# State-space kernel matrices shifted by selecting matmuls on TensorE, with the norm's weights multiplied into x by GpSimd

## Chip, cores and metric

One core of one Trainium2 chip. The metric is the device time of one execution in microseconds (us). Engines are called TensorE (PE in rows, its weight loads PEld), VectorE (DVE), ScalarE (ACT), GpSimd (POOL) and SyncE (SP), which issues most DMAs.

## What is computed

A two-layer encoder trunk on 256 positions of width 2048, in float32. Layer 0 mixes with an S5 state-space model (128 groups of 16 channels, each with 64 complex states), layer 1 with latent attention; each has a gated MLP with a short convolution. Every sub-layer stands between two RMS norms. The change lies in the first mixer:

```python
h = rmsnorm(x, norm_g[0, 0])            # x * rsqrt(mean(x*x) + eps) * g
# s5_mixer, per group of 16 channels:
x_re, x_im = einsum('blgp,gnp->blgn', ub, bb_re), einsum('blgp,gnp->blgn', ub, bb_im)
hs = scan over positions of h[t] = a * h[t-1] + x[t]        # complex, diagonal
y = einsum('blgn,gpn->blgp', hs_re, c_re) - einsum('blgn,gpn->blgp', hs_im, c_im) + d_skip * ub
y = gelu(y)
val, gate = split(y @ w_glu + b_glu, 2)
return val * sigmoid(gate)
```

## The kernel before

All matmuls with large weights split both operands into a rounded part and a remainder and sum three products (`mm3`, L108 to L110); ScalarE makes the rounded part `whi` and VectorE the remainder `wlo` (`split`, L73 and L74), from `raw`, which SyncE loads in pieces of 1 MB. The trunk runs through `s5`, the rest of the GLU, the MLP, attention and the second MLP in one stream; everything behind `s5` is dense in such matmuls.

`s5` cuts the 256 positions into 32 chunks of 8 and works on 8 channel groups at a time: 16 rounds, in a software pipeline. In round n, `part_a` for n + 1 builds on VectorE from powers of the state's eigenvalues (`z`) and the matrices B and C (`bc`) two products f1, f2 (output side) and e1, e2 (input side), each 128x1152 or 128x1024, and sums e1 and e2. B is first multiplied by the norm's weights (`g4`, loaded by SyncE for each round). `part_k` transposes the block of x into `U` (L442), multiplies the last two slices of e1 with f1 and f2 in column tiles of 32 (`tiled`, L399) and so gets one row block `K` of the kernel matrix within a chunk. The matrix within a chunk is a Toeplitz matrix, and its tile `TP` is K shifted by 16 columns for each of 8 rows of blocks. The shift is made by a round trip through DRAM: ScalarE's queue issues a DMA that writes K to `kd` (L460) and, when that has landed, a second one that reads it back with overlapping rows (L463):

```python
act.dma_start(kd.rearrange("r (j w) -> j r w", j=4), K.rearrange("p g c -> p (g c)"))
TPf = TP.rearrange("p j g c -> p (j g c)")[:, : RW - 112]
act.dma_start(TPf, bass.AP(kd.tensor, kd.offset + 16 * RW, [[16, 8], [RW, 16], [1, RW - 112]]))
```

`part_e` transposes e1 into `ET` (8 transposes, L471, copied by ScalarE). In round n + 1, `part_v` multiplies U by ET (L399), ScalarE copies that to `vs`, `part_r` transposes it (L487, L488), rotates it on VectorE (`co`, `si`) and runs the scan over chunks (L498), and `part_h` makes from it the states `H` at the chunks' starts (L503). In round n + 2, `part_c` sums U by TP and H by f1 and f2 into y (L399) and ScalarE applies the GELU into `yg`. After every fourth round `part_d` transposes yg (L540), and from then on each round can take one step of the GLU's matmuls (`glu_early`): 24 matmuls of 128x512, whose sums go to `f` (L256, L258).

At the start X is loaded (8 pieces), ScalarE squares it, GpSimd raises the mean to the power -1/2 (`rstd`, L121), and ScalarE scales X into `act` (`scale_x`, L347). A scheduler lays the instructions of each engine in a fixed order ahead of time; each engine runs its order strictly, and waits on semaphores where an operand isn't there.

## Time and profile before

| what | value |
|---|---|
| runs before, median of 3 | 2263.45 us (2258.99 to 2265.07) |
| the profiled execution, its time and its span | 2263.12 us, 2261.3 us |
| busy: TensorE, weight loads | 2087.9 us (92%), 1769.7 us (78%) |
| busy: VectorE, ScalarE, GpSimd | 1412.9 us (62%), 1095.6 us (48%), 76.5 us (3%) |
[...]
| moved by DMA | 393.28 MB, 174 GB/s |

The span is the time from the first to the last instruction of one profiled execution; its own time is 1.8 us longer. The busy shares are averages over stages that differ: the share of TensorE is far lower in the first 315 us than behind them. [...]

### The profile page before, as it was taken

How to read it: one execution, taken by the hardware profiler on the slowest of the kernel's cores; microseconds unless marked ns; L12 is line 12 of the kernel's file. 1: busy time of each engine (PE TensorE's matmuls, PEld its weight loads, DVE VectorE, ACT ScalarE, POOL GpSimd, SP SyncE). 2: the span in 40 equal slices, each digit the busy share in tenths (PEclk: the TensorE clock that was granted, in tenths of full speed). 3: DMA queues.
4: the chain of work that ended last, by engine and by line, in shares of the span. 5: the costliest groups of instructions: out<-in, count | busy, mean ns of one | idle time of the engine just before them, and what ended most of it. 6: DMA issues, size and time to landing. Idle time of an engine off the chain costs nothing. (4 is left out here: it accounts for less than half of the span.)

```text
span 2261.3 us, 30415 instructions
## 1 busy us (share of the span) xinstructions
PE 2087.9 (92%) x12244; PEld 1769.7 (78%) x12244; DVE 1412.9 (62%) x1904; ACT 1095.6 (48%) x1655; POOL 76.5 (3%) x93
## 2 busy tenths in 40 slices
PE   2576789899999999999998999989999999999997
PEld 1455567688888888888886899878888888888886
DVE  6777756666546655665667666476645655665566
ACT  5454434445545544553454455545545543554444
POOL 0000001200000000000002000120000000000001
PEclk9788899999999999999999999999999999999999
DMA  4455577646555555555555433545555555565554
GB/s 147 108 130 120 131 210 220 184 152 199 184 194 187 186 186 192 188 180 194 193 191 166 135 117 122 189 166 164 185 186 192 186 186 190 190 197 185 189 186 149
DMA packets 285245, 393.28 MB, mean 174 GB/s; under 512 B 9392, under 2 KB 198448, under 8 KB 284080
## 3 DMA queue, kind: packets, MB, share of 16 engines
q1 hardware_dynamic: 280816, 372.60, 50.8%
q10 hardware_dynamic: 4288, 18.74, 3.6%
q8 instruction: 96, 1.57, 0.3%
q14 instruction: 45, 0.37, 0.1%
HBM read 385.29 MB, written 6.03 MB: 173 GB/s over the span
## 5 line engine op out<-in xcount | busy, mean ns | idle before, releaser
L74 DVE TENSOR_TENSOR wlo<-raw,whi 128x1024 fp32r<-128x1024 f32 (+2 forms) x640 | 763.8, 1196 | 590.2 <-ACT whi L73 586.9
L73 ACT ACTIVATE whi<-raw 128x1024 fp32r<-128x1024 f32 (+2 forms) x640 | 658.0, 1031 | 646.5 <-PE wk L114 233.8
L114 PE MATMUL wk<-act,whi 128*128 128x512 f32 x2688 | 944.9, 396 | 0.0
L115 PE MATMUL wk<-act,wlo 128*128 128x256 f32 x2688 | 754.4, 281 | 0.0
L114 PEld LDWEIGHTS wk<-act,whi 128*128 128x128 f32 x2688 | 504.3, 188 | 121.0
L115 PEld LDWEIGHTS wk<-act,wlo 128*128 128x128 f32 x2688 | 507.9, 189 | 0.3
L109 PE MATMUL acc<-wlo,hh 128*128 128x512 f32 x652 | 255.8, 392 | 0.5
L108 PE MATMUL acc<-whi,hh 128*128 128x512 f32 x652 | 255.5, 392 | 0.0
L110 PE MATMUL acc<-whi,hl 128*128 128x512 f32 x652 | 254.4, 392 | 0.0
L109 PEld LDWEIGHTS acc<-wlo,hh 128*128 128x128 f32 x652 | 122.5, 188 | 28.5 <-DVE wlo L74 2.2
L108 PEld LDWEIGHTS acc<-whi,hh 128*128 128x128 f32 x652 | 122.5, 188 | 27.3 <-ACT hh L73 0.5
L110 PEld LDWEIGHTS acc<-whi,hl 128*128 128x128 f32 x652 | 122.5, 188 | 26.9
L109 PE MATMUL acc<-wlo,act 128*128 128x512 f32 (+1 forms) x332 | 129.6, 392 | 4.3 <-DVE wlo L74 4.2
L108 PE MATMUL acc<-whi,act 128*128 128x512 f32 (+1 forms) x332 | 130.0, 395 | 0.8 <-ACT act L73 0.4
L110 PE MATMUL acc<-whi,act 128*128 128x512 f32 (+1 forms) x332 | 127.3, 385 | 0.0
L166 POOL TENSOR_TENSOR f<-f,gb 128x512 f32<-128x512 f32 x24 | 38.1, 1593 | 1901.5 <-issue 1586.3
L109 PEld LDWEIGHTS acc<-wlo,act 128*128 128x128 f32 x332 | 65.0, 196 | 20.1 <-DVE wlo L74 8.2
L755 DVE SCALAR_TENSOR_TENSOR cv<-gs,cw,cv 128x255 f32<-128x255 f32 (+1 forms) x168 | 77.1, 480 | 3.0
L108 PEld LDWEIGHTS acc<-whi,act 128*128 128x128 f32 x332 | 64.7, 197 | 14.9 <-ACT whi L73 1.7
L110 PEld LDWEIGHTS acc<-whi,act 128*128 128x128 f32 x332 | 64.5, 194 | 11.3 <-issue 0.2
L753 ACT ACTIVATE cv<-gs,cb,cw 128x256 f32<-128x256 f32 x84 | 50.4, 601 | 36.7 <-DVE gs L705 36.7
L399 PE MATMUL wk<-TP,U 128*32 128x128 f32 x256 | 20.5, 369 | 47.4 <-DMA TP<-kd 42.5
(281 smaller groups left out, 2377.7 us busy)
## 6 DMA issues: line engine op xcount, KB each, us to landing
raw<-in_w_gate SPq DMA_DIRECT2D x88, 1024.0 KB
raw<-in_w_up SPq DMA_DIRECT2D x88, 1024.0 KB
raw<-in_w_down SPq DMA_DIRECT2D x88, 1024.0 KB
raw<-in_w_glu SPq DMA_DIRECT2D x32, 1024.0 KB
raw<-in_w_o SPq DMA_DIRECT2D x16, 1024.0 KB
TP<-kd ACTq DMA_DIRECT2D x16, 904.0 KB
raw<-in_w_ukv SPq DMA_DIRECT2D x8, 1024.0 KB
gb<-in_norm_g SPq DMA_DIRECT2D x6, 1024.0 KB
```

The costliest lines, as they stand in the source:

```text
L73: act.activation(hi, src, AF.Copy)
L74: (eng or dve).tensor_tensor(lo, src, hi.bitcast(F32), op=ALU.subtract)
L108: pe.matmul(o, lh, rh, start=first, stop=False)
L109: pe.matmul(o, lh, rl, start=False, stop=False)
L110: pe.matmul(o, ll, rh, start=False, stop=last)
L114: pe.matmul(ov, lh, r, start=first, stop=False)
L115: pe.matmul(ov[:, 0, :], ll, r[:, 0, :], start=False, stop=last)
L166: (dve if n == NCH - 1 else pool).tensor_tensor(c, c, g[0][:, n * 512 : (n + 1) * 512], op=ALU.mult)
L399: pe.matmul(o[32 * j : 32 * j + 32, g * P : (g + 1) * P], lhs(g, j), rhs(g, j), start=g == 0 and i == 0, stop=g == NG - 1 and i == len(ter ...
L753: act.activation(cv[:, ft, :], gv[:, ft, :], AF.Identity, scale=cw[:, 2, n : n + 1], bias=cb[:, n : n + 1])
L755: dve.scalar_tensor_tensor(cv[:, ft, sh:], gv[:, ft, : S - sh], cw[:, 2 - sh, n : n + 1], cv[:, ft, sh:], op0=ALU.mult, op1=ALU.add,)
```

## The change

Three edits, all in `s5`.

1. The round trip through DRAM goes. For each of four blocks of 32 columns (j), TensorE multiplies K, taken from a shifted column r, by a constant matrix of zeros and ones that selects 16 of K's rows (`C_SL` in `cst`, which grows from 638 to 894 columns): 2 x 2 x 2 x 4 = 32 matmuls into two banks, in column tiles of 32. ScalarE copies each bank into TP.
2. e1 and e2 are no longer summed on VectorE. `part_e` transposes both by matmuls with the identity that add up in the bank: 16 matmuls in place of 8 transposes. For `part_k` only the last slice is summed on VectorE, into `e7s`, whose other half is zero.
3. The norm's weights no longer go into B and into the skip matrix dB but into X: `gain_x`, 8 products of 128x4x128 on GpSimd in place. The loads of sG and the products with g4 and gX go.

```diff
+            e7s = [T(q1, [P, 8, 2, 16], F32, f"e7{i}", 1) for i in range(2)]
+            for z in e7s:
+                pool.memset(z[:, :, 0, :], 0.0)
...
-            dve.tensor_tensor(dB, dB, gX, op=ALU.mult)
...
+            def gain_x(qt):
+                c = slice(P * qt, P * qt + P)
+                for z in X:
+                    pool.tensor_tensor(z[:, :, c], z[:, :, c], gX[:, c].unsqueeze(1).to_broadcast([P, 4, P]), op=ALU.mult)
+
             def scale_x(rs, qt):
                 c = slice(P * qt, P * qt + P)
+                if qt:
+                    gain_x(qt)
...
-                g4 = T(q1, [P, NP, 16], F32, "g4")
-                sync.dma_start(g4.rearrange("p n q -> p (n q)"), a["sG"][sb].partition_broadcast(P))
-                dve.tensor_tensor(bc4[:, 0:2], bc4[:, 0:2], g4.unsqueeze(1).to_broadcast([P, 2, NP, 16]), op=ALU.mult)
...
-                dve.tensor_tensor(e1, e1, e2, op=ALU.add)
-                return e1, (f1, f2)
+                dve.tensor_tensor(e7s[sb % 2][:, :, 1, :], e1[:, :, 7, :], e2[:, :, 7, :], op=ALU.add)
+                return (e1, e2), (f1, f2)
...
-                    return flat2(e1[:, 4 * g + j, 6:8, :])
+                    return flat2(e7s[sb % 2][:, 4 * g + j])
...
-                act.dma_start(kd.rearrange("r (j w) -> j r w", j=4), K.rearrange("p g c -> p (g c)"))
-                TP = T(q1, [P, 4, NG, 240], F32, "TP")
-                TPf = TP.rearrange("p j g c -> p (j g c)")[:, : RW - 112]
-                act.dma_start(TPf, bass.AP(kd.tensor, kd.offset + 16 * RW, [[16, 8], [RW, 16], [1, RW - 112]]))
+                TP = T(q1, [P, 4, NG * P], F32, "TP")
+                for jj in range(2):
+                    bank = accb()
+                    for j in range(2):
+                        for odd in range(2):
+                            o = C_SL + (2 * (2 * jj + j) + odd) * 32
+                            for b in range(4):
+                                r = 16 * (2 * b + odd)
+                                pe.matmul(
+                                    bank[32 * b : 32 * b + 32, j * 256 : (j + 1) * 256].rearrange("p (g c) -> p g c", g=NG),
+                                    cst[:, o : o + 32], K[:, :, r : r + P],
+                                    start=j == 0 and odd == 0, stop=j == 1 and odd == 1, tile_position=(0, 32 * b),
+                                )
+                    act.activation(TP[:, 2 * jj : 2 * jj + 2, :], bank.rearrange("p (j c) -> p j c", j=2), AF.Copy)
...
-                        pe.transpose(ptv[:, g, :], e1[:, 4 * w + g].rearrange("p s q -> p (s q)"), ident)
+                        for i, z in enumerate(ee):
+                            pe.matmul(ptv[:, g, :], flat2(z[:, 4 * w + g]), ident, start=i == 0, stop=i == 1)
...
             z = [None]
+            gain_x(0)
             rs = first_norm()
```

The scheduler lays the orders anew. Three places show it.

TensorE, one round with a GLU step, from the last `e` tile (L399, now L408) on. In a row stand the bank and, behind the arrow, the moving and the stationary operand. Before:

```order
L110 MATMUL acc_1320<-whi_1315,act_212_925 128x512
...
L399 MATMUL wk_1403<-f_290_1293,e_291_1296 32x128 x4
L471 MATMUL wk_1427<-cst_73,e_291_1296 128x128 x4
L471 MATMUL wk_1433<-cst_73,e_291_1296 128x128 x4
L503 MATMUL wk_1439<-R_1396,cst_73 128x256
L399 MATMUL wk_1501<-ET_1426,U_1401 32x128 x4
L399 MATMUL wk_1513<-TP_1239,U_1216 32x128 x4
```

And of the change:

```order
L408 MATMUL wk_1490<-f_253_1388,e_46_183 32x128 x4
L486 MATMUL wk_1547<-cst_73,e_254_1391 128x128
L486 MATMUL wk_1547<-cst_73,e_255_1392 128x128
...
L472 MATMUL acc_1510<-K_44_179,cst_73 32x256 x16
L472 MATMUL acc_1528<-K_44_179,cst_73 32x256 x16
L486 MATMUL wk_1557<-cst_73,e_254_1391 128x128
...
L518 MATMUL wk_1567<-R_1483,cst_73 128x256
L108 MATMUL acc_1629<-whi_1621,act_214_1162 128x512
```

The selection stands in the middle of the transposed sums, and the GLU's matmuls moved from before the `e` tiles to behind part_h.

ScalarE, a round in which `frames` makes sines (`si`, `co`) for two rounds. Before:

```order
L384 ACT_TABLE_LOAD
L384 ACTIVATE si_1301<-si_1301,cst_73 128x512
L451 ACTIVATE K_44_181<-wk_1218 128x2x112
L472 ACTIVATE ET_1241<-wk_1242 128x512
L460 DMA kd_1237<-K_44_181 4x32x480
L472 ACTIVATE ET_1241<-wk_1248 128x512
L385 ACTIVATE co_1302<-co_1302,cst_73 128x512
L73 ACTIVATE whi_1465<-raw_1463 128x1024
L463 DMA TP_1239<-kd_1237 128x1x1808
L478 ACTIVATE vs_1356<-wk_1347 128x2x128
```

And of the change:

```order
L494 ACTIVATE vs_1858<-wk_1849 128x2x64
L393 ACT_TABLE_LOAD
L393 ACTIVATE si_2022<-si_2022,cst_73 128x512
L539 ACT_TABLE_LOAD
L539 ACTIVATE yg_1253<-wk_1861 128x2x8x16
L450 ACTIVATE U_1903<-wk_1900 128x256
L457 ACTIVATE K_44_179<-wk_1905 128x2x112
L394 ACT_TABLE_LOAD
L394 ACTIVATE co_2023<-co_2023,cst_73 128x512
L487 ACTIVATE ET_1961<-wk_1962 128x512
```

The two DMAs are gone; ahead of K's copy stand a sine, a GELU and two loads of function tables.

GpSimd at the start. Before:

```order
L143 MEMSET st_1736_9994 128x1
L121 ISA
L121 TENSOR_TENSOR rs_y_202<-rs_ms_200,cst_73 128x8
L357 MEMSET z_1261 128x32
L358 MEMSET z_1261 128x32
```

And of the change:

```order
L349 ISA
L349 TENSOR_TENSOR raw_94<-raw_94,gX_104 128x4x128 x4
L349 TENSOR_TENSOR raw_95<-raw_95,gX_104 128x4x128 x2
L121 TENSOR_TENSOR rs_y_205<-rs_ms_203,cst_73 128x8
L349 TENSOR_TENSOR raw_95<-raw_95,gX_104 128x4x128 x2
L366 MEMSET z_1574 128x32
```

Six of the eight products of X with the weights stand ahead of the norm's power, and two behind it.

## Rows read from the trace of the kernel before

**Rows 1.** Windows: us, busy PE, PEld, DVE, ACT, POOL, clock, DMA share, GB/s.

```profile
33.00:104.00 71.00, 39.72 (x544) 29.86 (x545) 49.09 (x82) 26.91 (x64) 0.18 (x2) 0.74 0.47 124
104.00:305.00 201.00, 142.84 (x1455) 108.63 (x1454) 145.00 (x230) 89.88 (x179) 0.22 (x3) 0.82 0.56 133
...
315.00:2261.00 1946.00, 1895.39 (x10164) 1623.84 (x10162) 1188.65 (x1524) 949.94 (x1334) 72.63 (x69) 0.99 0.55 181
```

**Rows 2.** Timeline of VectorE: the scans (L498), one a round; start, duration.

```profile
42.81 0.68 DVE L498 TENSOR_TENSOR_SCAN R<-dc,w 128x256 f32<-128x256 f32 x1
...
103.78 0.69 DVE L498 TENSOR_TENSOR_SCAN R<-dc,w 128x256 f32<-128x256 f32 x1
...
304.51 0.68 DVE L498 TENSOR_TENSOR_SCAN R<-dc,w 128x256 f32<-128x256 f32 x1
```

**Rows 3.** Waits of TensorE from 36 to 320 us: total, times, longest.

```profile
PE wk L399 <- DMA TP<-kd: 42.5, 12, 8.6
PE wk L399 <- ACT ET L472: 15.2, 6, 7.1
PE wk L487 <- ACT vs L478: 15.0, 7, 4.8
```

**Rows 4.** Waits of ScalarE in the same stretch.

```profile
ACT vs L478 <- DMA kd<-K: 22.6, 4, 9.3
ACT bc L420 <- DMA bc<-in_sBC: 21.3, 3, 9.8
```

**Rows 5.** Windows, a stretch in which TensorE waits.

```profile
50.00:55.00 5.00, 0.08 (x4) 0.11 (x8) 0.00 (x0) 0.00 (x0) 0.00 (x0) 0.50 0.45 106
```

**Rows 6.** Timeline of TensorE, a dense stretch.

```profile
158.44 1.08 PE L399 MATMUL wk<-f,e 128*32 128x128 f32 x32
159.46 1.09 PE L471 MATMUL wk<-cst,e 128*128 128x128 f32 x8
160.38 0.38 PE L503 MATMUL wk<-R,cst 128*128 128x256 f32 x1
```

**Rows 7.** Timeline of TensorE from 284 to 296 us.

```profile
286.56 0.60 PE L503 MATMUL wk<-R,cst 128*128 128x256 f32 x2
...
287.23 0.39 PE L109 MATMUL acc<-wlo,act 128*128 128x512 f32 x1
287.46 0.40 PE L110 MATMUL acc<-whi,act 128*128 128x512 f32 x1
...
293.03 0.43 PE L399 MATMUL wk<-TP,U 128*32 128x128 f32 x8 [2.55 <-DMA TP<-kd]
...
294.48 0.50 PE L109 MATMUL acc<-wlo,act 128*128 128x512 f32 x1
```

**Rows 8.** Timeline of VectorE at the start.

```profile
20.99 0.17 DVE L123 TENSOR_TENSOR rs_t<-rs_y 128x8 f32<-128x8 f32 x1 [1.55 <-POOL rs_y L121]
...
25.57 1.35 DVE L430 TENSOR_TENSOR f<-z,bc 128x1152 f32<-128x1152 f32 x1
...
31.64 1.22 DVE L435 TENSOR_TENSOR e<-e,e 128x1024 f32<-128x1024 f32 x1
```

**Rows 9.** Timeline of TensorE at the start: the first `e` tiles.

```profile
32.91 1.93 PE L399 MATMUL wk<-f,e 128*32 128x128 f32 x32 [7.70 <-DVE e L435]
```

**Rows 10.** Groups by line up to 250 us: busy, mean ns of one, idle before.

```profile
L472 ACT ACTIVATE ET<-wk 128x512 f32<-128x512 f32 x26 | 14.8, 594 | 3.8 <-PE wk L471 1.8 <-DVE w L505 1.0 <-DVE w L506 0.4
...
L524 ACT ACT_TABLE_LOAD x5 | 6.4, 1283 | 10.5 <-DMA kd<-K 9.6 <-issue 0.8
...
L418 DVE TENSOR_TENSOR bc<-bc,g 128x256 f32<-128x256 f32 x15 | 6.3, 417 | 0.0
```

**Rows 11.** Timeline of VectorE and GpSimd from 343 us, products in SBUF.

```profile
341.97 1.22 DVE L74 TENSOR_TENSOR wlo<-raw,whi 128x1024 fp32r<-128x1024 f32 x1 [1.05 <-ACT whi L73]
...
343.20 1.75 POOL L166 TENSOR_TENSOR f<-f,gb 128x512 f32<-128x512 f32 x1 [215.28 <-DMA x<-in_x]
...
344.05 1.98 DVE L74 TENSOR_TENSOR wlo<-raw,whi 128x1024 fp32r<-128x1024 f32 x1 [0.26 <-ACT whi L73]
```

## The prediction

> **What bounds the kernel now.** Read the table of windows first. From 315 us on TensorE is busy 1895 of 1946 us at a clock of 0.99, and the change touches nothing there; from 33 to 305 us it is busy 39.7 of 71 and 142.8 of 201 us, at 0.74 and 0.82 [rows 1]. That stretch is the state-space layer, 16 rounds of `part_a` to `part_h`, and it is where the change lives. One scan per round marks the pace: the first at 42.8, the fifth at 103.8, the sixteenth at 304.5 us [rows 2], so 15.2 us a round at first and 18.2 us later. The waits say why: TensorE stands 42.5 us for the tile TP, which comes back from DRAM, 15.2 for ET and 15.0 for vs [rows 3]. ScalarE makes ET and vs, and it stands itself, because TP's second DMA is in its queue behind the first one's landing: 22.6 us before vs alone, and 21.3 for bc [rows 4]. So of the 90 us of TensorE's idleness most comes from the round trip. [...]

> **What the change costs TensorE.** [...] Part_c's 48 tiled records take 1.45 and a matmul of the GLU 0.23; a full-width fp32 matmul of 256 columns is two records, and with the next one they take 0.67, so 0.22 each [rows 7], twice a transpose's 128 columns.
> - The transposes of e1 become 16 matmuls, each two records of 128 columns: 32 x 0.11 = 3.5 instead of 0.9, +2.6 us a round.
> - The selection is 32 matmuls in 64 records of 128x32, with 256 moving columns. The nearest row has the same tile shape and 128 columns at 0.03; twice that, less the fixed part, is 0.056: 64 x 0.056 = 3.6 us. Below that it can't be had (its columns double), above it the bound is 0.22 each, no overlap of column tiles at all.
> - A round is then: `e` tiles 1.0, transposed sums 3.5, selection 3.6, part_h 0.4, part_v 0.5, part_c 1.45, six transposes 0.65, and 0.4 for changes of tile shape (the first matmul behind one lasts 0.50, not 0.39 [rows 7]): 11.5 us, of which 6.2 is new. With a GLU step (24 x 0.23 = 5.5) it is 17.0. GLU steps lie in rounds 5 to 8, 10 to 13 and 15 to 17: rounds 9 and 14 only find their generator empty.

> **What it takes away.** Both DMAs of a round and the waits for them; on VectorE the sum of e1 and e2 (1.22 [rows 8]; 0.2 comes back for the slice that e67 needs) and the product of bc (0.42 [rows 10]). VectorE is busy 145.0 us in the eleven rounds from the fifth scan [rows 1]; less 11 x 1.6 that is 11.6 a round, so its saving lies beside TensorE's 17 and is worth nothing there; if TensorE were faster, VectorE would be next. The loads of sG leave SP's queue, which was not the one waited for: nothing. ScalarE gets two copies of TP at 0.6 [rows 10] and loses two DMA issues; the order has 19 loads of function tables in this layer where there were 13, at 1.28 each [rows 10]. ScalarE's 89.9 us [rows 1] are 8.2 a round, and 1.2 for the copies and half a table load make 10, again beside TensorE.

> **New waits in a round.** The selection needs K, so TensorE now stands where only a DMA stood. In the order 4 to 8 transposed sums (0.9 to 1.8 us) lie between the `e` tiles and the selection. K is behind, on ScalarE, yg and U, and in every other round a sine and two table loads; on VectorE behind a product of 1.3 us. I get 0.3 us of waiting in a plain round and 1.7 in one with the sine: 1.0 on average. In the four rounds of the first GLU block vs also queues behind f's copy and a split: 0.35. Without a GLU step nothing covers vs, ET and yg: 1.3 a round.

> **The start.** The products with the norm's weights go to GpSimd, eight of 128x512 at about 1.7, and where GpSimd multiplies, a VectorE product with both inputs in SBUF stands: one of 1.22 took 1.98, ending 1.1 behind GpSimd's [rows 11]. GpSimd's power for the norm was done at 21.0 [rows 8]; now six of the eight products are ahead of it in GpSimd's queue, and VectorE's whole queue stands behind that power. With the first at some 13 us, when the squares of X have been read, 13 + 6 x 1.75 and 1.9 for the power make 25.4, and with 1 more for VectorE's turns I put its result at 26.5 (bounds 21, if all fitted ahead of it, and 29). From there to the first f it was 4.6 us; now 3.9 without two bc products, and 2.4 more for the two products left. The f and e products took 7.3, now 6.2. So the first `e` tiles begin at 39 instead of 32.9 [rows 9]: **+6**. Then the first round has its tiles at the lower clock (2.0, as in [rows 9]), 10 records of sums at 0.21, the selection 3.6, 22 records 2.4, and ET, vs and the rotation 5.5: first scan at 55, **12 us late**.

> **The sum.** First to fifth scan: 11.5 + 3 x 12.8 = 50 instead of 61: -11. Fifth to sixteenth: nine GLU rounds of 17.0 + 0.2 for part_d + 1.15 of waiting = 18.35, and two without of 13.4: 192 instead of 200.7: -8.7. Behind it the last wait for TP, 1.4 at most, goes. Together 12 - 11 - 8.7 - 1 = -8.7. The profiled execution has a span of 2261.3 and took 2263.1; its time is 0.3 below the median of the runs, so I set **2255 us**. About 0.3%, 6.8 us, is what a measurement tells from no change, so the gain barely clears it: 100 us of new TensorE work buys 90 us of waits and some 40 us of slow clock (TensorE is busy 182 us from 33 to 305 us for some 140 of work at the upper level: 15 rounds of 5.0, ten GLU steps, 3 x 0.9 and a start).

> **Rivals.**
> - **K's wait decides (slower, 2280).** If each round's selection stands one table load more, 1.28 + 0.3, behind ScalarE's queue, 16 x 1.6 = 26 us come back: 2280. For it: TensorE's order no longer has GLU matmuls in front of the wait. Against: ScalarE is no longer held by DMAs. From 1.0 + 8.7/16 = 1.5 us of waiting a round there is no gain. 22%.
> - **Waits hidden (faster, 2239).** The 1.0 to 1.3 us a round do not appear, -16. For it: that the reading of the order behind them takes every queue at its worst place. Against: K's chain crosses two engines in every round. 12%.
> - **The wait was not the round trip's (no change, 2263).** bc's load keeps its 21.3 us: it is issued behind a free buffer. That eats the gain. 15%.
> - **Column tiles do not overlap (slower, 2309 or more).** A selection record at a full-width price of 0.11 gives 64 x 0.11 = 7.0, +54 us; at 0.22, +168. Against: 32 loads and 32 matmuls, all on 128 rows, take 1.02 us [rows 6], which only overlap allows. 3%. [...]
> [...]

> **How the numbers follow.** The forecast has 45%, its own range 2246 to 2264 (start 8 to 15 us late, 0.6 to 1.6 us of waiting): two thirds of that is faster by over 0.3%, 0.30, and 0.15 within. Faster: 0.30 + 0.12 = 0.42. Within: 0.15 + 0.15 = 0.30. Slower: 0.22 + 0.03 + 0.03 = 0.28. The range from 2238 to 2286 takes in the hidden waits and K's wait with some spread, and leaves out the two costly tile cases, 6%, and some 12% at the two ends.

> **What would show it.** Right: no wait for TP, no kd; 64 selection records in 3.5 to 4 us; a clock near 1.00 from 60 to 300 us; TensorE over 90% busy there; the first scan at 53 to 57, the fifth near 105, the sixteenth near 296. Wrong: selection records spaced 0.1 or more; waits for K above 1.5 us a round; a first scan behind 60 or before 48; the clock still falling to 0.50 between rounds.

## The result, and the profile after the change

The changed kernel takes **2249.86 us** (median of 9 runs, 2246.36 to 2254.62), the kernel before 2262.69 us (median of 9 runs beside them, 2258.99 to 2277.39). The ratio is 0.9939, 95% interval 0.9919 to 0.9958: 0.6% faster. The forecast was 2255 (2238 to 2286), with faster as the likeliest case. The profiled execution of the change took 2254.62 us and has a span of 2252.8, so its span is 8.5 us shorter than that of before; it is the longest of its nine runs, 4.8 above their median.

The windows of the kernel after, over the state-space layer and behind it (columns as in [rows 1]; the clock is the granted TensorE clock as a share of full speed, over the whole execution 0.967 before and 0.989 after):

```profile
33.00:104.00 71.00, 60.90 (x921) 45.90 (x924) 57.41 (x97) 42.45 (x105) 0.18 (x2) 0.98 0.23 68
104.00:305.00 201.00, 195.08 (x2572) 152.50 (x2563) 134.79 (x218) 117.22 (x214) 0.22 (x3) 1.00 0.21 63
315.00:2252.00 1937.00, 1888.12 (x10124) 1619.14 (x10122) 1181.43 (x1514) 946.07 (x1329) 71.76 (x69) 0.99 0.55 180
```

Compared with [rows 1], TensorE went from 142.8 to 195.1 busy of 201 us and its clock from 0.82 to 1.00; DMA share fell from 0.56 to 0.21. The stretch is now TensorE's: it stands 6 of 201 us. VectorE has 10 us less to do and ScalarE 27 more. So 52 us more of TensorE's time, measured at a higher clock, replace idleness, and the layer gets only a little shorter.

The scans on VectorE's timeline after, first, fifth and sixteenth (they answer to [rows 2]):

```profile
56.49 0.68 DVE L513 TENSOR_TENSOR_SCAN R<-dc,w 128x256 f32<-128x256 f32 x1
...
105.82 0.69 DVE L513 TENSOR_TENSOR_SCAN R<-dc,w 128x256 f32<-128x256 f32 x1
...
295.11 0.69 DVE L513 TENSOR_TENSOR_SCAN R<-dc,w 128x256 f32<-128x256 f32 x1
```

The first scan is 13.7 us later than before, the next four rounds win 11.6 back (49.3 us instead of 61.0), and the eleven behind them win 11.4 (189.3 instead of 200.7). So the sixteenth scan comes 9.4 us earlier (295.11 instead of 304.51).

What TensorE waits for after, 36 to 320 us (answers to [rows 3]; total, times, longest):

```profile
PE wk L408 <- DVE e L441: 6.7, 1, 6.7
PE wk L486 <- DVE w L506: 3.2, 5, 1.1
PE wk L502 <- ACT vs L493: 1.8, 5, 0.5
PE wk L408 <- ACT ET L487: 1.5, 2, 1.0
```

The 42.5 us for TP are gone, and so are nearly all of the 15 each for ET and vs. The longest wait left is the one at the start, for the first `e` tiles. For K only TensorE's weight loads (PEld) stand, in three rounds and for 0.7 us in all:

```profile
PEld acc L472 <- DVE K L458: 0.7, 3, 0.3
```

What VectorE and ScalarE wait for in the same stretch, the longest sums of each:

```profile
DVE e L439 <- PE wk L486: 35.8, 10, 4.8
DVE wlo L74 <- ACT whi L73: 25.7, 16, 4.7
...
ACT whi L73 <- PE acc L110: 31.3, 17, 5.1
ACT TP L477 <- PE acc L472: 17.6, 14, 2.6
...
ACT bc L425 <- DMA bc<-in_sBC: 6.0, 6, 1.4
```

The direction has turned round: VectorE waits for the transposed sums to read e before it may overwrite it, and ScalarE no longer waits for the landing of kd [rows 4] but for TensorE's banks. Its wait for the load of bc went from 21.3 us [rows 4] to 6.0.

One round without a GLU step, on TensorE's timeline after (a record's duration includes its overlap with the next, for the selection 180.55 + 3.66 = 184.21 where the next start is 184.14, so the spacing of the starts is what it costs):

```profile
174.62 0.64 PE L408 MATMUL wk<-ET,U 128*32 128x128 f32 x16
...
177.31 1.08 PE L408 MATMUL wk<-f,e 128*32 128x128 f32 x32
178.60 2.02 PE L486 MATMUL wk<-cst,e 128*128 128x128 f32 x16 [0.21 <-DVE w L506]
180.55 3.66 PE L472 MATMUL acc<-K,cst 128*32 128x256 f32 x64
184.14 2.05 PE L486 MATMUL wk<-cst,e 128*128 128x128 f32 x16
186.03 0.60 PE L518 MATMUL wk<-R,cst 128*128 128x256 f32 x2
...
187.43 0.64 PE L408 MATMUL wk<-ET,U 128*32 128x128 f32 x16
```

The 64 selection records take 3.59 us from their first start to the next instruction's (180.55 to 184.14), 0.056 each. The load of one selecting matrix lasts longer than that (shortest, median and longest time in ns):

```profile
L472 PEld LDWEIGHTS acc<-K,cst x1024: 106/110/110, 44.1 to 281.8; 128*32 128x32 f32 x171
```

The 32 records of the transposed sums take 1.95 + 1.89 = 3.84. The round is 12.8 us long and has one visible wait, of 0.21.

The start, on GpSimd's and VectorE's timelines after (the last row of the first view is from one that ends at 18.6 us, where the first of the six products stands alone):

```profile
13.36 11.72 POOL L349 TENSOR_TENSOR raw<-raw,gX 128x512 f32<-128x512 f32 x6 [10.90 <-DMA dB<-in_dX]
25.05 1.65 POOL L121 TENSOR_TENSOR rs_y<-rs_ms,cst 128x8 f32<-128x8 f32 x1
26.67 2.48 POOL L349 TENSOR_TENSOR raw<-raw,gX 128x512 f32<-128x512 f32 x2
...
13.36 5.35 POOL L349 TENSOR_TENSOR raw<-raw,gX 128x512 f32<-128x512 f32 x1 [10.90 <-DMA dB<-in_dX]
```

```profile
17.10 0.28 DVE L313 SCALAR_TENSOR_TENSOR L<-L 128x128 f32<-128x128 f32 x1
...
17.72 1.27 DVE L312 TENSOR_TENSOR uu<-L 128x256 f32<-128x256 f32 x1
18.91 1.35 DVE L313 SCALAR_TENSOR_TENSOR L<-L 128x128 f32<-128x128 f32 x1
20.18 1.34 DVE L316 TENSOR_TENSOR L<-uu 128x128 f32<-128x128 f32 x1
26.73 1.22 DVE L123 TENSOR_TENSOR rs_t<-rs_y 128x8 f32<-128x8 f32 x1 [5.20 <-POOL rs_y L121]
...
33.41 1.35 DVE L436 TENSOR_TENSOR f<-z,bc 128x1152 f32<-128x1152 f32 x1
```

The power for the norm comes out of GpSimd at 26.7 instead of 21.0 [rows 8], because six products stand ahead of it, and VectorE stands 5.2 us for it. GpSimd is busy all the time from 13.4 to 25.1 us, but not evenly: its first product takes 5.35 us and the other five 1.3 to 1.4 each. During most of the first one VectorE's products keep their usual time (0.28 us for 128x128 at 17.10); from 17.72 on, three of them take 1.27 to 1.35, where 128x128 had taken 0.28. So at first GpSimd's product is the long one and then VectorE's are; what decides between them no run here shows. The first f starts at 33.4 instead of 25.6 [rows 8], TensorE's first `e` tiles at 39.9 instead of 32.9 [rows 9].

### The profile page after: what moved, and what is told of

It reads as the page before. It is cut to its first block, busy times and chain, and to the rows that moved or that the text cites. A ratio compares the mean times of both kernels' runs of the same rounds, so it can differ in the third digit from the quotient of the medians.

```text
span 2252.8 us, 33157 instructions
## 1 busy us (share of the span) xinstructions
PE 2155.2 (96%) x13652; PEld 1826.6 (81%) x13652; DVE 1402.3 (62%) x1887; ACT 1125.5 (50%) x1695; POOL 89.9 (4%) x103
## 3 DMA queue, kind: packets, MB, share of 16 engines
q8 instruction: 107, 1.75, 0.3%
## 5 line engine op out<-in xcount | busy, mean ns | idle before, releaser
L108 PE MATMUL acc<-whi,act 128*128 128x512 f32 (+1 forms) x332 | 126.4, 381 | 2.1 <-ACT whi L73 1.6
L109 PE MATMUL acc<-wlo,act 128*128 128x512 f32 (+1 forms) x332 | 125.0, 377 | 3.4 <-DVE wlo L74 3.4
L110 PE MATMUL acc<-whi,act 128*128 128x512 f32 (+1 forms) x332 | 124.2, 375 | 0.0
L486 PEld LDWEIGHTS wk<-cst,e 128*128 128x128 f32 x512 | 61.3, 196 | 13.7 <-issue 11.3
L486 PE MATMUL wk<-cst,e 128*128 128x128 f32 x512 | 67.3, 286 | 3.3 <-DVE w L506 3.2
```

What stands on the lines that cost most here:

```text
L108: pe.matmul(o, lh, rh, start=first, stop=False)
L109: pe.matmul(o, lh, rl, start=False, stop=False)
L110: pe.matmul(o, ll, rh, start=False, stop=last)
L486: pe.matmul(ptv[:, g, :], flat2(z[:, 4 * w + g]), ident, start=i == 0, stop=i == 1)
```

## The experiments

The theory to be tested is the prediction's: the round trip was the wait, TensorE becomes the bound, VectorE's saving is worth nothing beside it, GpSimd's products cost the start. The rivals were that summing in the transposes or the work on GpSimd is what pays, or that something else paces the rounds. Each of the three edits was tried alone on the kernel before; then the change with one edit undone. The scheduler lays the orders anew in every one of them, so a difference of a few us can be the new order's; no run separates that.

**1. The selection alone.** Edit (kernel before, with the change's selection; e1 and e2 summed on VectorE, weights in B):

```diff
-                kd = T(dp, [32, RW], F32, "kd")
-                act.dma_start(kd..., K...)
...
-                act.dma_start(TPf, bass.AP(kd.tensor, ...))
...
+                for jj in range(2):
+                    ...
+                                pe.matmul(bank[...], cst[:, o : o + 32], K[:, :, r : r + P], ...)
+                    act.activation(TP[:, 2 * jj : 2 * jj + 2, :], ..., AF.Copy)
```

> The kernel before with the selecting matmuls alone: e1 and e2 are summed on VectorE and transposed once, and the norm's weights stay in B. Theory (after the change TensorE's own work sets the pace of the rounds): a round costs TensorE 2.6 us less than in the changed kernel, and GpSimd's products at the start are gone. First scan at 46 to 48 us, fifth near 91, sixteenth near 248 (GLU rounds of 14.9, VectorE at 13.2 just below); time 2205 us, 2193 to 2217. Rival 1 (VectorE's relief is what paid): slower than the changed kernel's 2250, near 2258. Rival 2 (less DMA traffic paid, TensorE is not the bound): the same as the changed kernel, 2246 to 2252.

Measured: **2210.77 us**, ratio 0.9765 (0.9744 to 0.9786), 53 us faster than before and 39 faster than the whole change. Its windows from the fifth scan to the sixteenth and from the first to the fifth, and its longest waits on TensorE:

```profile
92.90:255.20 162.30, 152.64 (x2141) 111.48 (x2142) 138.19 (x220) 110.10 (x203) 0.22 (x3) 1.00 0.25 72
48.10:92.90 44.80, 37.68 (x711) 25.61 (x709) 44.43 (x76) 27.21 (x62) 0.18 (x2) 1.00 0.19 49
```

```profile
PE wk L495 <- ACT vs L486: 6.5, 4, 3.1
PE acc L466 <- DVE K L452: 5.5, 7, 1.9
```

Eleven rounds take 162.3 us instead of 189.3, TensorE 94% busy in them and VectorE 85%. In the first four rounds, which have no GLU step, VectorE is busy 44.4 of 44.8 us, so there it is the bound. Here a wait for K does appear, 5.5 us in seven rounds: only the 8 transposes, some 1 us, lie ahead of the selection there, where the change has 8 to 26 records of its sums, 1.1 to 3.2 us.

**2. The summed transposes alone.** Edit (kernel before; e2 also gets a second buffer, as in the change, which the lines below leave out):

```diff
-                dve.tensor_tensor(e1, e1, e2, op=ALU.add)
+                dve.tensor_tensor(e7s[sb % 2][:, :, 1, :], e1[:, :, 7, :], e2[:, :, 7, :], op=ALU.add)
...
-                        pe.transpose(ptv[:, g, :], e1[...], ident)
+                        for i, z in enumerate(ee):
+                            pe.matmul(ptv[:, g, :], flat2(z[:, 4 * w + g]), ident, start=i == 0, stop=i == 1)
```

> The kernel before with the sum of e1 and e2 in the transposes alone; the round trip and the weights in B stay. Theory: TensorE gets 42 us of work, but in rounds in which it waits for DMAs; most is covered: 2263 to 2275. Rival 1 (VectorE's relief paid): 2245 to 2255, since 16 x 1.2 us of VectorE go.

Measured: 2255.17 us, ratio 0.9963 (0.9951 to 0.9975): 8 us faster, at the upper edge of rival 1, where the theory had a loss. So the theory's 42 us of new TensorE work (16 x 2.6) do not show in the kernel with the round trip. Its window, and its waits for vs, ET and TP:

```profile
104.00:305.00 201.00, 166.40 (x1854) 137.93 (x1854) 134.39 (x221) 94.90 (x182) 0.22 (x3) 0.91 0.58 128
```

```profile
PE wk L491 <- ACT vs L482: 19.0, 12, 3.6
PE wk L402 <- ACT ET L476: 16.6, 6, 4.6
PE wk L402 <- DMA TP<-kd: 10.8, 5, 3.7
```

TP's wait fell from 42.5 [rows 3] to 10.8 although its DMAs are the same: TensorE fills the time with its own new work, at a clock of 0.91 instead of 0.82. Two readings were left: it is TensorE's added work that raises the clock and pays for itself (A), or it is VectorE's sum, gone from each round's chain (B). Experiments 7 and 8 try each alone.

**3. The weights on GpSimd alone.** Edit (kernel before):

```diff
+            def gain_x(qt):
+                ...
+                    pool.tensor_tensor(z[:, :, c], z[:, :, c], gX[:, c]..., op=ALU.mult)
...
-                dve.tensor_tensor(bc4[:, 0:2], bc4[:, 0:2], g4..., op=ALU.mult)
```

> The kernel before with the norm's weights multiplied into X by GpSimd alone. Theory: the first e tiles start 6 us later, the rounds keep their pace: 2264 to 2272. Rival 1 (VectorE's relief paid): 16 x 0.4 us less on VectorE outweigh the start, 2255 to 2260.

Measured: 2263.11 us, ratio 0.9998 (0.9985 to 1.0011): no change, just below the theory's range and above the rival's. Its first scan is at 49.60 instead of 42.81 [rows 2] and its sixteenth at 307.32 instead of 304.51, so the start is 6.8 us late and 4.0 of that are won back in the rounds, where VectorE has 0.42 us less.

**4. No shift at all.** Edit (kernel before; TP is a tile set to zero once, so y's part within a chunk is left out):

```diff
+            TPs = [T(q1, [P, 4, 2, 240], F32, f"TP{i}", 1) for i in range(2)]
+            for z in TPs:
+                pool.memset(z, 0.0)
...
-                kd = T(dp, [32, RW], F32, "kd")
-                act.dma_start(kd..., K...)
-                TP = T(q1, [P, 4, NG, 240], F32, "TP")
-                act.dma_start(TPf, bass.AP(kd.tensor, ...))
+                TP = TPs[sb % 2]
```

> The kernel before without the shift: TP is set to zero once and never loaded, so the part of y from within a chunk is left out, and both DMAs of a round with it. It measures what the round trip costs in full. Theory: the rounds go at VectorE's pace, 13.2 us, fifth scan near 85, sixteenth near 232, the clock near 1.00 in dense rounds; 2190 us, 2178 to 2205. So the wait is worth 70 us, and the change gave 57 of it back as TensorE work. Rival 2 (bc's load and other waits take the place): 2225 or more.

Measured: 2188.52 us, ratio 0.9669 (0.9649 to 0.9688). The round trip was worth **75 us**, and nothing else had to be touched to get them. They include whatever its queue and its traffic cost other transfers; ScalarE's wait for bc, for one, falls from 21.3 us [rows 4] to 6.1. Of the 75 the selection alone (experiment 1) keeps 53: its 16 x 3.6 = 58 us of TensorE work cost 22. The window from the fifth scan (81.69) to the sixteenth (234.25) and the longest wait on TensorE show why not all 58:

```profile
81.70:234.20 152.50, 124.68 (x1443) 93.21 (x1442) 143.56 (x229) 89.65 (x175) 0.22 (x3) 0.97 0.30 84
```

```profile
PE wk L402 <- DVE e L438: 24.7, 8, 7.5
```

Without the trip VectorE is the bound, 94% busy where TensorE is busy 82%, and its sum of e1 and e2 (L438) is what TensorE waits for. Part of the selection's work falls into that idle time: the eleven rounds take 162.3 us with it (experiment 1) and 152.5 here, the first scan comes at 48.1 instead of 42.0, the four rounds between take 44.8 instead of 39.7. That is 9.8 + 6.1 + 5.1 = 21 of the 22 us.

**5. The change without GpSimd's products** (the weights back in B, on VectorE):

```diff
-            gain_x(0)
...
+                dve.tensor_tensor(bc4[:, 0:2], bc4[:, 0:2], g4..., op=ALU.mult)
```

> The changed kernel with the norm's weights back in B (their load and VectorE's product in each round) and out of GpSimd. Theory: the rounds stay TensorE's, so VectorE's 0.4 us are hidden; the start is 7 us earlier, first scan near 48 to 50; 2243 us, 2240 to 2247. Rival (the product of bc is on the path): 2250 or more.

Measured: 2242.16 us, ratio 0.9894 (0.9868 to 0.9921). Undoing this edit wins 7.7 us. Its scans are at 48.23, 97.15 and 286.40: the first 8.3 us earlier than in the change, the rounds equally long (189.25 us from the fifth to the sixteenth, against 189.29). In that stretch:

```profile
97.15:286.40 189.25, 183.62 (x2420) 143.18 (x2414) 129.31 (x211) 112.61 (x206) 0.22 (x3) 1.00 0.21 61
```

TensorE is busy 97% of it and VectorE 68%. GpSimd's products cost the start their 8 us, and the product of bc that they save on VectorE is worth nothing in the rounds.

**6. The change without the summed transposes** (e1 and e2 summed on VectorE, transposed once):

```diff
...
-                            pe.matmul(ptv[:, g, :], flat2(z[:, 4 * w + g]), ident, start=i == 0, stop=i == 1)
+                        pe.transpose(ptv[:, g, :], e1[...], ident)
```

> The changed kernel with e1 and e2 summed on VectorE and transposed once. Theory: 2.6 us less of TensorE in 16 rounds, VectorE just below it, and the late start stays: 2211 to 2220, 4 us above the kernel with the selection alone. Rival 1 (VectorE's relief pays): 2255 or more.

Measured: 2218.11 us, ratio 0.979 (0.9758 to 0.9821). Undoing the summed transposes wins **32 us**; its first scan is at 55.84, as late as in the change, and its sixteenth at 262.46 instead of 295.11. Between experiments 1 and 5, which have no products on GpSimd, the same edit costs 31 us. So the price of the summed transposes on top of the selection is the same with and without GpSimd's products.

**7. TensorE's part of the summed transposes alone** (kernel before, VectorE's sum kept; each transpose becomes two matmuls, the second one's operand a tile of zeros):

```diff
-                        pe.transpose(ptv[:, g, :], e1[...], ident)
+                        for i, z in enumerate((flat2(e1[:, 4 * w + g]), ez)):
+                            pe.matmul(ptv[:, g, :], z, ident, start=i == 0, stop=i == 1)
```

> The kernel before, round trip and all, in which each transpose becomes two matmuls with the identity, the second one of a tile of zeros; VectorE sums e1 and e2 as before. So TensorE has the work of the summed transposes without the relief of VectorE. Theory A (more work keeps TensorE's clock up, which pays): near the 2255 of the sum alone. Theory B (the relief of VectorE shortens the way from a wait's end to the next one): 2266 to 2280.

Measured: 2261.93 us, ratio 0.9984 (0.9969 to 1.0): no change that can be told. Neither theory's number came. The window and the waits:

```profile
104.00:305.00 201.00, 163.90 (x1814) 134.96 (x1813) 144.34 (x228) 96.29 (x189) 0.22 (x3) 0.90 0.54 124
```

```profile
PE wk L490 <- ACT vs L481: 27.2, 11, 4.7
...
PE wk L401 <- DMA TP<-kd: 6.2, 3, 2.4
```

TensorE is busy 21 us more in this window than before, at 0.90 instead of 0.82, and from 36 to 320 us the wait for TP shrinks by 36 us while that for vs grows by 12. That the time stays the same is the sum of two opposite effects, as the scans show: the fifth comes at 116.27, 12.5 us late, and the eleven rounds behind it take 189.0 us instead of 200.7, which wins 11.7 back. The loss begins in the first round, on ScalarE and TensorE:

```profile
45.08 0.60 ACT L475 ACTIVATE ET<-wk 128x512 f32<-128x512 f32 x1 [3.74 <-DMA kd<-K]
45.73 0.43 PE L401 MATMUL wk<-ET,U 128*32 128x128 f32 x8 [4.12 <-ACT ET L475]
```

The doubled transposes last from 35.78 to 41.18 us there, 5.4 us where the transposes of before take 1.9 (34.78 to 36.68), and the copy of ET's second half now stands behind the landing of kd in ScalarE's order; in the kernel before it ran at 36.78, ahead of that wait. So the doubled transposes are free in sum only. Without VectorE's relief they do not give experiment 2's gain, but they shorten the eleven rounds; whether the clock, the new order or the moved waits do that is not separated.

**8. VectorE's part alone** (kernel before; VectorE sums only the last slice, TensorE transposes e1 alone, so e2 is left out of ET; e2 has its second buffer, but VectorE alone touches it):

```diff
-                dve.tensor_tensor(e1, e1, e2, op=ALU.add)
+                dve.tensor_tensor(e7s[sb % 2][:, :, 1, :], e1[:, :, 7, :], e2[:, :, 7, :], op=ALU.add)
...
-                        pe.transpose(ptv[:, g, :], e1[:, 4 * w + g].rearrange("p s q -> p (s q)"), ident)
+                        pe.transpose(ptv[:, g, :], flat2(ee[0][:, 4 * w + g]), ident)
```

> The kernel before, round trip and all, in which VectorE sums only the last slice and TensorE transposes e1 alone: e2 is left out of ET, so part of the states is left out. VectorE is relieved as in the sum alone, TensorE has no more work than before. Theory A (the clock pays): 2260 to 2265. Theory B (VectorE's relief pays): 2240 to 2252.

Measured: 2243.88 us, ratio 0.9898 (0.9874 to 0.9923). So B holds: in the kernel with the round trip relieving VectorE of the sum is worth about 20 us. VectorE's own time is less by 15 us (16 x 1.22 [rows 8], less 16 x 0.28 for the slice that is still summed); where the other 5 come from is not shown. The window and the wait for TP:

```profile
104.00:305.00 201.00, 149.34 (x1536) 113.23 (x1535) 142.84 (x240) 94.51 (x188) 0.22 (x3) 0.85 0.58 144
```

```profile
PE wk L402 <- DMA TP<-kd: 52.6, 14, 8.3
```

The wait for TP is longer than before, 52.6 instead of 42.5, and the kernel is faster: by the code each round's chain is sum, `e` tiles, K, DMA out, DMA back, and the sum is 1.22 us of it. That TensorE, freed earlier too, arrives at the wait earlier still would explain the longer wait; it was not tried by itself. Experiments 7 and 8 do not add up to experiment 2 (about 0 and -20 against -8). The scans of the three traces show where (us against before, [rows 2]):

| experiment | first scan | the four rounds behind it | the eleven behind those | sixteenth scan |
|---|---|---|---|---|
| 2, both parts | +7.1 | -0.3 | -14.4 | -7.6 |
| 7, TensorE's part | +7.7 | +4.8 | -11.7 | +0.8 |
| 8, VectorE's part | -0.6 | -1.1 | -15.9 | -17.7 |

The late start comes with TensorE's part. In the eleven rounds each part alone wins 12 to 16 us and both together 14, so there the two gains overlap almost wholly; which wait they share is not shown.

**9. The selection twice** (the change, with every selecting matmul issued twice into the same sums, so TP comes out doubled):

```diff
-                        for odd in range(2):
+                        for rep, odd in ((0, 0), (0, 1), (1, 0), (1, 1)):
```

> The changed kernel with every selecting matmul issued twice into the same sums (TP comes out doubled), so that only TensorE gets more work: 64 more selection records a round, 3.66 us by the changed kernel's own row. Theory (TensorE is the bound from the first scan to the sixteenth, its rounds have no slack): 16 rounds x 3.6 = +58 us, 2300 to 2310, first scan about 60, sixteenth about 353. Rival (another engine or a chain of waits paces the rounds and TensorE's matmuls have slack): less than half of it, below 2280. If the selection costs more in place than its 3.66 us (weight loads that don't overlap with neighbours, a change of tile shape): above 2315.

Measured: 2300.1 us, ratio 1.017 (1.0146 to 1.0193), 50 us more than the change, at the lower edge of what the theory said; its scans come 3 and 8 us earlier than the theory had them. From the first scan (57.40) to the sixteenth (345.19):

```profile
57.40:345.20 287.80, 282.12 (x4173) 210.14 (x4172) 161.63 (x268) 141.16 (x265) 0.40 (x5) 1.00 0.15 43
```

That is 49.2 us longer than the same stretch of the change (238.6), and TensorE is busy 50.7 us longer (231.4 there). One more selection costs 49.2 / 15 = 3.3 us a round where its row says 3.6: the rounds have hardly any slack. Added TensorE work turns into time nearly one for one.

**The account.** All against before: the selection gives -53 (what the missing trip gives, -75, less 22). On top of it the summed transposes cost +31 and GpSimd's products +8; together -14, where the medians measured -13 and the ratio -14. These steps lead from the kernel before to the change one by one, so they must add up; what tests them is the other way round, by experiment 6: GpSimd's products on the selection alone cost 7 us (2218 against 2211), the summed transposes on top of them 32. The best kernel of the study is the selection alone, at 2211 us.

## Why the prediction was right, step by step

- **The bound.** Right: the round trip was the wait. Experiment 4 prices it at 75 us, where the prediction spoke of most of 90 us of idleness. The rival that bc's load keeps its 21.3 us is out: 6.0 are left after the change.
- **Selection, 64 x 0.056 = 3.6 us.** Right: 3.59 in the trace, 3.3 more a round when it is done twice. The 0.03 that it doubles is [rows 6], 32 records in 1.02 us; the fixed part that it takes off is in no row, and 0.056 is what was measured. The rival of column tiles that do not overlap is out: all tiles use all 128 rows, and a weight load of 0.110 us came every 0.056 us.
- **Transposed sums, 32 x 0.11 = 3.5 us.** Slightly small: 3.84, 0.12 each. Per round the extra was put at 2.6; experiments 1 and 5 differ by (189.3 - 162.3) / 11 = 2.5 of elapsed time. The trace shows 0.24 us for a matmul of two records where a transpose takes 0.115 (0.92 for 8, [rows 6]), a factor of 2.1. The other of the two costly cases at 3% each, sums far dearer than two records of 0.11, did not come.
- **A round, 17.0 and 11.5 us without waits, 18.35 and 13.4 with them.** A GLU round without waits takes 17.3 in the trace (157.30 to 174.62), one without a GLU step 12.8, and the nine GLU rounds then average (189.3 - 2 x 12.8) / 9 = 18.2. **The term that was mis-sized is the waiting in a round**, "1.0 on average" for K. The waits for K come to 0.7 us in the whole layer, and all idleness from the fifth to the sixteenth scan is 189.3 - 183.5 = 5.8 us, 0.5 a round, where the sum had about 14. The error of the other sign is TensorE's work, 183.5 us where the sum had 178 (9 x 17.2 + 2 x 11.5): among it 0.35 a round for the sums. Together the stretch took 189.3 instead of 192, nearer than either part: that two errors of opposite sign almost cancel is luck. The rival of hidden waits was half right, therefore, and K's wait as the thing that decides is out.
- **VectorE's saving "is worth nothing there".** Right in the changed kernel as far as it was tried: experiment 5 shows that 0.42 us more on VectorE in each round change nothing. The sum's own 1.22 were not put back alone; that VectorE waits 35.8 us for TensorE there speaks for the same. But the prediction did not see that in the kernel before VectorE was part of the round's chain: the same saving is worth 20 us there (experiment 8). It was right because the selection had already taken the bound to TensorE.
- **The start, +6 for the `e` tiles and +12 for the first scan.** The tiles came at 39.9 instead of 39, the scan at 56.5 instead of 55: +13.7. GpSimd's power was put at 26.5 and was ready at 26.7, which is partly luck: six products at 1.75 were expected, and one of 5.35 and five of 1.3 came. Experiment 5 says that this is not all GpSimd's: without its products the first scan is at 48.2, still 5.4 late, as it is with the selection alone (48.1), so the first round's selection takes the rest. No run shows the 0.21 for a record of the first round's sums: ten took 2.31 us (41.79 to 44.10), 0.23 each. The tiles took 1.87 (39.92 to 41.79). The granted clock was 1.00 in both stretches, so the lower clock that the prediction names there is not shown either.
- **The sum, -8.7.** The two profiled executions differ by 8.5 us, the medians by 12.8 and the ratio says 13.8 (9.5 to 18.3). By scans it is +13.7 - 11.6 - 11.4 = -9.4 (before rounding) where the prediction had +12 - 11 - 8.7. The signs that it named came: no wait for TP, a clock of 0.98 to 1.00, and the three scans at 56.5, 105.8 and 295.1 where it had 53 to 57, 105 and 296. The profiled execution of the change is the longest of its nine, so part of the 4 us between sum and median is spread between executions; how much can't be read from one trace.
- **The sentence that "100 us of new TensorE work buys 90 us of waits and some 40 us of slow clock"** holds roughly. From 33 to 305 us TensorE's idleness falls from 89.4 to 16.0 us, so 74 of the 90 were bought; its busy time there rises by 73, of which some 9 are work that used to come later, so of 100 us of new work some 36 were paid by the faster clock, as an estimate from these rows. What a slow clock costs stands in the trace of before: at a granted 0.50 (152.2 to 154.4 us) the GLU's matmuls start 0.43 us apart, at 1.00, the prediction's upper level (154.5 to 158.0), 0.23. But the sentence hid the main point: of the two kinds of new TensorE work, the selection's 58 us buy the waits and the clock, and the sums' 42 us buy nothing. Two edits of a diff were costed in one sum, and the sum being right said nothing about whether each was worth having.
- **Smaller slips.** The saving on VectorE is put at 1.6 us a round, where the prediction's own 1.22 - 0.2 + 0.42 make 1.44. A round without a GLU step is 12.8 in one place and 13.4 in the other, and the 0.6 between them is not derived. The trace has 21 loads of function tables in the layer, not 19. None of them moves the forecast by more than 2 us.

## What to carry to other kernels

When one edit of a change moves the bound to another engine, price the other edits against the new bound, not the old one: relief for VectorE was worth 20 us before the round trip was gone, and cost 31 us as work on TensorE once it was. Work that an engine does in time it would have waited is free only as long as the wait is there: the doubled transposes cost nothing in sum in one kernel, and in the other 31 us even with VectorE's relief. A time that stays the same can hide a loss and a gain, which the scans of experiment 7 tell apart. And a queue that is idle on average, here GpSimd at 3%, is not free at the one place where the start of everything stands behind it (8 us, experiment 5).
